# Two heads at a time, 36 chunks of layer 0 beside the choice and spread of experts, and layer 1 with 64 tokens by gathered rows

## The chip, the core and the metric

The kernel runs on one core of a Trainium2 chip. The metric is the device time of one execution in microseconds (us). The core has TensorE (PE, with its weight loads shown as PEld), VectorE (DVE), ScalarE (ACT), GpSimd (POOL) and SyncE (SP, which here only issues DMAs), and 16 DMA engines which all queues share.

## The reference

Two layers work on 256 context tokens and 256 latent tokens of 1024 values. Layer 0 mixes tokens by latent attention (8 heads) and a retention (8 heads), layer 1 by a gated delta rule. After each mixer comes a "peer" layer, a product-key mixture of 16384 experts, each one row of `u` and one row of `v`:

```python
def peer(h, w_q, k1, k2, u_tab, v_tab):          # per block of 128 tokens xb
    q = (xb @ w_q).reshape(PEER_BLOCK, PEER_HEADS, 2, half)
    s1 = jnp.einsum('phd,hnd->phn', q[:, :, 0], k1); s2 = jnp.einsum('phd,hnd->phn', q[:, :, 1], k2)
    v1, i1 = lax.top_k(s1, PEER_TOPK); v2, i2 = lax.top_k(s2, PEER_TOPK)
    ...
    sc, j = lax.top_k(cand, PEER_TOPK)            # 16 experts of each of 8 heads
    gate = jax.nn.softmax(sc.astype(F32), axis=-1)
    act = jax.nn.gelu(jnp.einsum('phkd,pd->phk', u_tab[e_idx], xb).astype(F32), approximate=False)
    return jnp.einsum('phk,phkd->pd', (gate * act).astype(xb.dtype), v_tab[e_idx])
```

So each token has 128 slots (8 heads, 16 experts). In layer 0 all 512 tokens go through `peer`, in layer 1 only the 256 latent ones.

## The kernel before

All arithmetic is float32. Where accuracy allows one pass, a factor is split into a high and a low part (`split`, L264: ScalarE rounds to the high part at L270, VectorE or GpSimd subtracts at L273), and a product is three matmuls of such parts (`mm3`, L258; each `mm` is at L256). Other products are plain f32 matmuls, which the trace shows as two instructions each.

**Layer 0's mixer** (`mixer0`). After the projections, a pipeline of eight `attend(h)` is woven with a pipeline of four `retain(hp)`. A head of attention makes queries and keys (tiles `q`, `k`), scores `s`, a softmax, transposes `pt` to `pT`, and at the end the product `oa`: 64 columns of weights (`VM`) against `pT`, so a head fills one half of the columns of the array and of the rows of the output, by h % 2. Retention takes heads in pairs, one after the other: scores `rs` with 64 rows of the array, product with a decay on VectorE to `sd`, and the product `or` with 64 columns.

**The peer layers** are done densely and by rows. Dense: the experts stand in 128 chunks of 128. For a chunk, `act` (24 matmuls, a chunk of `u` as weights, N tokens as columns) gives the activations of all tokens against all experts of the chunk, `gelu` follows, they are multiplied by the weight matrix W (zero where a token did not choose the expert), and `f` adds the product with the chunk of `v` into PSUM (per block of 128 tokens two halves of 512 columns, three matmuls each). Layer 0 does three of four token blocks so (N = 384), layer 1 both (N = 256).

W is made by `route`. *Choice*: the projections `pq`, scores `sc`, and on VectorE the top 16 of each half and of the candidates. *Spread*: `decode`, `place`, `slots`, and `spread`, which for groups of 16 tokens builds one-hot tiles `O` and `A` on VectorE and ScalarE, multiplies them (`wp`, 32 matmuls per group) and writes the result `wst` to W in DRAM. `EARLY` = 12 and 24 chunks of `act` of layers 0 and 1 are woven into the spread, and their activations stay in SBUF.

`Dense.run` then goes over pairs of chunks: `act` of both (if not early), the extra work listed in `fill` for these chunks, the loads of W (`w`, four chunks at a time) and of `vr`, `gelu` times W (L1108), splits of the activations (`gsh`, `gsl`) and of `vr` (`vsh`, `vsl`), and the products `f` of the pair before. `ur` and `vr` have two buffers each, the split `vs` three in layer 0 and four in layer 1.

*Rows* (layer 0, the last block of 128 tokens): `Rows.steps` goes over 128 slots. A step gathers one row of `u` for each of the 128 tokens by an indirect DMA of GpSimd (L1042), takes the product with the token on VectorE (L1049), and eight steps later adds the gathered row of `v` times its weight (L1059). These steps, and 56 units that compute the modulation (`ada_unit`, L343: one load of 512 KB, one or two passes of VectorE), are spread over the chunks of layer 0's loop by `fill`: steps from chunk 8 to 120, units at every second chunk from chunk 12.

The build orders the instructions of each engine; a few of a later chunk can stand ahead of their place in the code. Queues run in order: SyncE's holds the loads of `ur`, `vr`, `w` and `adat`, GpSimd's the gathers.

## Time and profile before

| what | value |
|---|---|
| time, median of 3 runs | 3143.77 us (3142.84 to 3145.04) |
| the profiled execution | 3142.63 us, of which span 3140.7 us |
| mean granted TensorE clock | 0.94 |
| busy: TensorE, VectorE, ScalarE, GpSimd | 2816.7, 2305.4, 1281.7, 708.5 us |
| DMA | 626 MB, mean 199 GB/s |

Stages in the span: layer 0's mixer to 390, choice and spread of layer 0 to 690, its dense loop to 1745, the delta rule to 2245, choice and spread of layer 1 to 2436, its dense loop to 3123, the end to 3140.7. The share of a busy engine is read per stretch: "busy" of TensorE is the time in which some matmul is open, and matmuls overlap, so the number of them in a stretch says more on the pace. The chain of work that ended last shows what each instant waited for.

### The profile page before, as it was taken

The numbers are of one execution on the slowest core, as the hardware profiler recorded it, in microseconds if no ns is written. First come the engines' busy times: TensorE is split into PE (matmuls) and PEld (weight loads), VectorE is DVE, ScalarE is ACT, GpSimd is POOL, SyncE is SP. The second block draws the span as 40 slices with busy tenths as digits, with TensorE's granted clock in tenths as the row PEclk, the third lists the DMA queues.
The fourth block names the chain that finished last, engine by engine and source line by source line (L and its number), as shares of the span: only waits on it lengthen the run. The fifth ranks groups of instructions, "written<-read, shape, count | busy, mean of one in ns | idle before, by whom it ended". The sixth has DMA issues, their size and how long they took to land.

```text
span 3140.7 us, 44585 instructions
## 1 busy us (share of the span) xinstructions
PE 2816.7 (90%) x16843; PEld 2443.3 (78%) x16843; DVE 2305.4 (73%) x4520; ACT 1281.7 (41%) x2145; POOL 708.5 (23%) x453
## 2 busy tenths in 40 slices
PE   8989895857999999999999887669887899999997
PEld 4756685746999998888999666668787689999997
DVE  2955689977999999994444587976799655555555
ACT  3234432753333333333333334322348454444443
POOL 2410130024545555540000234423310100000000
PEclk9999997978999999999999888779899899999999
DMA  6530321568999999994443122312336866667663
GB/s 229 187 108 21 114 75 61 198 245 307 378 382 380 384 397 400 400 362 156 156 156 118 57 63 78 95 48 81 115 128 237 264 216 210 213 210 213 210 213 108
DMA packets 257192, 626.02 MB, mean 199 GB/s; under 512 B 34800, under 2 KB 124016, under 8 KB 252496
## 3 DMA queue, kind: packets, MB, share of 16 engines
q1 hardware_dynamic: 217632, 478.58, 45.3%
q0 software_dynamic: 38768, 142.49, 11.7%
q8 instruction: 132, 2.16, 0.3%
q10 hardware_dynamic: 576, 2.10, 0.2%
q14 instruction: 84, 0.69, 0.1%
HBM read 574.86 MB, written 48.23 MB: 198 GB/s over the span
## 4 chain that ended last, share of the span: by engine, by line
PE 55%; DVE 27%; DMA 9%; issue 5%; ACT 3%; POOL 1%; SPq 0%; POOLq 0%; ACTq 0%; DVEq 0%
PE f L256 20%; PE act L256 20%; DMA ur<-p_u 3%; DMA vr<-p_v 3%; DVE adaj L343 2%; DVE usl L273 2%; DVE cv L1264 2%; PE dz L256 1%; DVE O L966 1%; DVE rowy L1059 1%; PE y L256 1%; DVE vsl L273 1%; DVE rowu L1049 1%; DVE gelu L1108 1%; PE s L256 1%
## 5 line engine op out<-in xcount | busy, mean ns | idle before, releaser
L256 PE MATMUL f<-vsh,gsh 128*128 128x512 f32 x1260 | 491.1, 395 | 36.0 <-ACT vsh L270 36.0
L256 PE MATMUL f<-vsl,gsh 128*128 128x512 f32 x1260 | 497.7, 395 | 12.7 <-DVE vsl L273 12.5
L256 PE MATMUL f<-vsh,gsl 128*128 128x512 f32 x1260 | 494.9, 393 | 0.0
L273 DVE TENSOR_TENSOR vsl<-vr,vsh 128x1024 fp32r<-128x1024 f32 x252 | 301.4, 1228 | 246.8 <-ACT vsh L270 246.3
L273 DVE TENSOR_TENSOR usl<-ur,ush 128x1024 fp32r<-128x1024 f32 x256 | 313.5, 1226 | 173.9 <-ACT ush L270 173.9
L270 ACT ACTIVATE vsh<-vr 128x1024 fp32r<-128x1024 f32 x252 | 256.6, 1053 | 339.1 <-PE f L256 233.9
L270 ACT ACTIVATE ush<-ur 128x1024 fp32r<-128x1024 f32 x256 | 270.4, 1056 | 280.3 <-PE act L256 210.4
L256 PE MATMUL act<-hp0h,usl 128*128 128x384 f32 x1024 | 346.0, 338 | 14.5 <-DVE usl L273 14.5
L256 PE MATMUL act<-hp0h,ush 128*128 128x384 f32 x1024 | 347.0, 339 | 0.6 <-ACT ush L270 0.6
L256 PE MATMUL act<-hp0l,ush 128*128 128x384 f32 x1024 | 345.4, 337 | 0.0
L256 PEld LDWEIGHTS f<-vsh,gsh 128*128 128x128 f32 x1260 | 239.0, 190 | 88.8 <-ACT vsh L270 42.1
L256 PE MATMUL act<-hp1h,usl 128*128 128x256 f32 x1024 | 293.6, 287 | 7.7 <-DVE usl L273 7.7
L256 PE MATMUL act<-hp1h,ush 128*128 128x256 f32 x1024 | 293.6, 287 | 5.5 <-ACT ush L270 5.5
L256 PE MATMUL act<-hp1l,ush 128*128 128x256 f32 x1024 | 292.2, 285 | 0.0
L256 PEld LDWEIGHTS f<-vsl,gsh 128*128 128x128 f32 x1260 | 239.3, 190 | 65.4 <-DVE vsl L273 19.2
L256 PEld LDWEIGHTS f<-vsh,gsl 128*128 128x128 f32 x1260 | 239.1, 190 | 49.6
L270 ACT ACTIVATE gsh<-gelu 128x384 fp32r<-128x384 f32 (+1 forms) x256 | 120.3, 471 | 376.4 <-DVE gelu L1108 342.3
L1042 POOL DMA_INDIRECT rowu<-p_ur,rowe x128 | 181.6, 1419 | 189.7 <-DVE rowa L1049 135.3
L1042 POOL DMA_INDIRECT rowv<-p_v,rowe x128 | 180.2, 1408 | 146.0 <-DVE rowy L1059 121.4
L256 PEld LDWEIGHTS act<-hp0h,usl 128*128 128x128 f32 x1024 | 193.8, 189 | 15.7 <-DVE usl L273 15.3
L256 PEld LDWEIGHTS act<-hp1h,usl 128*128 128x128 f32 x1024 | 199.1, 195 | 8.9 <-DVE usl L273 8.7
L256 PEld LDWEIGHTS act<-hp1h,ush 128*128 128x128 f32 x1024 | 198.9, 194 | 8.4 <-ACT ush L270 6.3
(770 smaller groups left out, 5970.8 us busy)
## 6 DMA issues: line engine op xcount, KB each, us to landing
ur<-p_u SPq DMA_DIRECT2D x256, 512.0 KB, 4.4
vr<-p_v SPq DMA_DIRECT2D x256, 512.0 KB, 4.4
adat<-ada_t SPq DMA_DIRECT2D x80, 512.0 KB, 7.1
W<-wst SPq DMA_DIRECT2D x20, 2048.0 KB, 7.1
w<-W SPq DMA_DIRECT2D x32, 768.0 KB, 9.5
wq<-p_wq SPq DMA_DIRECT2D x32, 512.0 KB, 3.4
dw<-dn_in SPq DMA_DIRECT2D x32, 512.0 KB, 3.4
w<-W SPq DMA_DIRECT2D x32, 512.0 KB, 5.6
```

Source lines behind the costliest of these rows:

```text
L256: self.nc.tensor.matmul(out, l, r, start=start, stop=stop)
L270: nc.scalar.activation(hi, x, AF.Copy)
L273: (eng or nc.vector).tensor_sub(lo, x, hi.bitcast(F32))
L343: nc.vector.tensor_tensor_reduce(j, w, self.crow[:, s, :], op0=ALU.mult, op1=ALU.add, scale=1.0, scalar=self.c["ada_c"][:, l, m, k:k + 1], ...
L966: nc.vector.tensor_tensor(pairs(O[:, n]), bc(n), iob.unsqueeze(1).broadcast_to([P, OH, 64, 2]), ALU.is_equal)
L1042: nc.gpsimd.indirect_dma_start(t, None, tabs[z], bass.IndirectOffsetOnAxis(ap=self.e[:, s:s + 1], axis=0))
L1049: nc.vector.tensor_tensor_reduce(u, u, self.h, op0=ALU.mult, op1=ALU.add, scale=1.0, scalar=0.0, accum_out=self.act[:, s:s + 1])
L1059: nc.vector.scalar_tensor_tensor(self.y, rows.pop((1, v)), self.g[:, v:v + 1], self.y, ALU.mult, ALU.add)
L1108: nc.vector.tensor_mul(gv, gv, w4[:, :, c % WC, :])
L1264: (nc.gpsimd if CONV[j] == "p" else nc.vector).scalar_tensor_tensor(co, xp[:, :ns, q:q + T], cw[:, j, q:q + 1], co, ALU.mult, ALU.add)
```

## The change

Three things. **Heads two by two:** `attend` of an even head stops after its transposes, and the odd head's `oa` does both heads, alternating between the halves of the array; `retain` makes `rs` and `or` of its two heads alternating. **Layer 0, 36 chunks early:** `EARLY` is 36 and 24; activations of all but the first `KEEP` = 4 early chunks are written to DRAM (`away`, ScalarE's queue) and read back in the loop (SyncE's queue). The early work now begins in the choice, once the projections are issued (`step`), where GpSimd makes the low parts; it goes on between `decode`, `place` and in `spread`; the four kept chunks come last. The next chunk's table is loaded and split while the present one is multiplied. The `fill` work of the loop is placed by shares of its cost (`paces`): the units and the affine step earlier, the row steps from about chunk 32 to the end. **Layer 1:** 192 tokens dense (`N` = P + HALF), the last 64 by rows. Both halves of the partitions hold these tokens, with slots 0 to 63 and 64 to 127, so 64 steps gather two slots at a time. Of the weighted rows every second is added on TensorE in f32 (`halves`, weights `d` made by ScalarE), the others on VectorE (`rowy`), which a last product folds. For the half block, `gs` holds high and low parts side by side, so that `f` needs two matmuls instead of three there. The tables are the same data under two names.

```diff
-EARLY = 12, 24
-LEAD = 15, 45
+EARLY = 36, 24
+KEEP = 4
-RING = 4, 3
+RING = (4, 3), (4, 3)
@@ attend(h)
-            o = ps.tile([P, T2], F32, tag="ps", name=f"oa{h}")
+            if h % 2 == 0:
+                first.append(pTs)
+                return
+            both = (first.pop(0), pTs)
...
                 for kb in range(nk):
-                    self.mm(o[rows, s * T:(s + 1) * T], VM[:, kb, h * 64:(h + 1) * 64], pTs[s][:, kb, :], kb == 0, kb == nk - 1)
-            put(h // 2, rows, o[rows])
+                    for z in range(2):
+                        self.mm(o[z * 64:z * 64 + 64, s * T:(s + 1) * T], VM[:, kb, (h - 1 + z) * 64:(h + z) * 64], both[z][s][:, kb, :], kb == 0, kb == nk - 1)
+            put(h // 2, slice(0, P), o)
@@ retain(hp)
+            for s, b0, own in ((0, 0, 0), (1, 0, 1), (1, 2, 0)):
+                os = [ps.tile([P, 2, T], F32, tag="ps", name=f"rs{hp}{z}{s}{b0}") for z in range(2)]
+                for sb in range(2):
+                    k0 = (b0 + sb) * P
+                    for z in range(2):
+                        self.mm(os[z][:, sb, :], rk[rows[z], hp, k0:k0 + P], rq[rows[z], hp, s * T:(s + 1) * T])
...
-        rest = pipe([retain(hp) for hp in range(4)], 2)
+        rest = pipe([retain(hp) for hp in range(4)], 2, 3)
@@ route
+        pd, work = dense.p, dense.early(e2, ps)
+        beside = islice(work, (EARLY[l] - KEEP) * KD // 2)
...
+        def step(n):
+            for _ in range(n):
+                next(beside, None)
...
+                if ends[0]:
+                    n += 1
+                    step(1 + n % 2)
                 yield
...
+            step(4 + 4 * l)
...
-            for gi in range(P // OH):
+            for gi in range(min(P, dense.N - tb * P) // OH):
...
-                weave(spread(tb, SHARE[l]), until=work)
+                weave(spread(tb, SHARE[l]), until=beside)
         weave(work)
@@ Rows.choose, halves, steps
+                    for r in range(0, P, self.n):
+                        for z in range(2):
+                            self.m.mm(o[r:r + self.n, i * P:(i + 1) * P], hs[z][:, 4 * h + i, ts].bitcast(F32), c["ident"], z == 0, z == 1)
...
+        def halves(self, acc, w, t, first, last):
+            for h in range(2):
+                self.m.mm(acc[h * 64:h * 64 + 64, :], w, t[:, h * 512:(h + 1) * 512], first, last)
...
+                    if acc is not None and v % 2 == 0:
+                        d = pool.tile([P, n], F32, tag="rowd", name=f"rowd{l}{v}", bufs=3)
+                        nc.scalar.activation(d, self.fold, AF.Copy, scale=self.g[:, v:v + 1])
+                        self.halves(acc, d, t, v == 0, False)
+                    else:
+                        nc.vector.scalar_tensor_tensor(self.y, t, self.g[:, v:v + 1], self.y, ALU.mult, ALU.add)
@@ Dense
+        def ahead(self, order, ps):
+            m, nc, l = self.m, self.m.nc, self.l
+            us = self.table(order[0])
+            for n, c in enumerate(order):
+                now, us = us, None
+                o = ps.tile([P, 512], F32, tag="ps", name=f"act{l}{c}")
+                for k in range(KD):
+                    self.product(o, now, k)
+                    if k == 1 and n + 1 < len(order):
+                        us = self.table(order[n + 1])
+                    if k % 2:
+                        yield
+                if c < KEEP:
+                    self.gelu(c, o)
+                else:
+                    g = self.pg.tile([P, self.N], F32, tag="gelus", name=f"gelus{l}{c}", bufs=3)
+                    nc.scalar.activation(g, o[:, :self.N], AF.Gelu)
+                    nc.scalar.dma_start(self.away[c], g)
...
+            def fetch(c):
+                late = c >= NE - 2
+                vr = (self.p if late else pool).tile([P, D], F32, tag="ur" if late else "vr", name=f"vr{l}{c}", bufs=2)
+                nc.sync.dma_start(vr, m.a[f"p_vr{l}"][c * P:(c + 1) * P])
+                if KEEP <= c < done:
+                    self.gelu(c, None)
+                return vr
...
+                        if half:
+                            for z in range(2):
+                                m.mm(acc[tb][h], gs[:, whole:whole + P], vs[z][:, hl], first and z == 0, last and z == 1)
+                        else:
+                            m.mm3(acc[tb][h], (gs[:, sl], gs[:, second(tb * P):second(tb * P) + P]), (vs[0][:, hl], vs[1][:, hl]), first, last)
@@ build
+        def paces(done, first, second):
+            cost = np.cumsum([second if c < done else first + second for c in range(NE - 6)])
+            return lambda share: int(np.searchsorted(cost, min(share, 1.0) * cost[-1]))
...
+        fill, at = {}, paces(EARLY[0], 18, 18)
+        ahead_share = EARLY[0] / (2 * (NE - 6) - EARLY[0])
         for i, u in enumerate(units):
-            fill.setdefault(12 + 2 * i, []).append(lambda u=u: m.ada_unit(pa, *u))
+            n = 3 * KD
+            share = ahead_share * (0.1 + 0.9 * i / n) if i < n else ahead_share + (0.97 - ahead_share) * (i - n) / (len(units) - n)
+            fill.setdefault(at(share), []).append(lambda u=u: m.ada_unit(pa, *u))
...
-            fill.setdefault(8 + i * 112 // (P + LAG), []).append(lambda: next(steps))
+            fill.setdefault(at(0.9 * ahead_share + (1 - 0.9 * ahead_share) * i / (P + LAG)), []).append(lambda: next(steps))
...
+            dense = m.Dense(m, 1, h, P + HALF, *pools1, EARLY[1])
...
+            fill, at = {2: [affine]}, paces(EARLY[1], 24, 20)
+            for i in range(rows.n + LAG):
+                fill.setdefault(at((i + 1) / (rows.n + LAG)), []).append(lambda: next(steps))
```

## Rows read from the trace of the kernel before

**Rows 1.** The page's part 4: shares of the chain that ended last, by engine.

```profile
PE 55%; DVE 27%; DMA 9%; issue 5%; ACT 3%; POOL 1%; SPq 0%; POOLq 0%; ACTq 0%; DVEq 0%
```

**Rows 2.** Stretches: length, busy PE, PEld, DVE, ACT, POOL (instructions), PEclk, DMA, GB/s.

```profile
196.00:331.00 135.00, 130.74 (x585) 82.60 (x585) 78.95 (x163) 60.85 (x133) 0.00 (x0) 1.00 0.14 42
495.00:690.00 195.00, 130.84 (x1145) 116.65 (x1143) 183.56 (x367) 113.52 (x252) 2.79 (x4) 0.84 0.46 175
690.00:772.00 82.00, 50.36 (x183) 38.43 (x183) 59.03 (x74) 24.57 (x33) 45.35 (x27) 0.76 0.83 291
772.00:1044.00 272.00, 271.41 (x1373) 247.20 (x1374) 271.32 (x383) 99.17 (x143) 138.12 (x98) 1.00 1.01 377
1044.00:1420.00 376.00, 365.89 (x1836) 330.01 (x1836) 356.47 (x496) 130.07 (x191) 197.89 (x139) 1.00 1.01 384
...
2304.00:2436.00 132.00, 104.20 (x981) 96.72 (x980) 127.39 (x236) 88.23 (x189) 0.58 (x1) 0.90 0.52 192
```

**Rows 3.** Groups, 196 to 331, TensorE: tile, shapes, count | busy us, mean ns.

```profile
L256 PE MATMUL rs<-rq,rk 64*128 64x256 f32 x96 | 27.6, 407 | 0.0
...
L256 PE MATMUL oa<-pT,VM 128*64 128x256 f32 x96 | 21.3, 382 | 0.0
```

**Rows 4.** Timeline of TensorE: start us, length us, instruction, count merged.

```profile
233.99 0.38 PE L256 MATMUL oa<-pT,VM 128*64 128x256 f32 x1
234.05 0.38 PE L256 MATMUL or<-sd,rv 128*64 128x256 f32 x1
234.21 0.38 PE L256 MATMUL oa<-pT,VM 128*64 128x256 f32 x1
...
237.32 2.80 PE L256 MATMUL or<-sd,rv 128*64 128x256 f32 x12
```

**Rows 5.** The chain in order of time: start us, us, matmuls packed, count.

```profile
307.66 0.86 PE gm L256 x2
403.44 0.89 PE sc L256 x8
550.57 3.41 PE wp L256 x32
846.55 8.34 PE act L256 x48
854.89 8.20 PE f L256 x36
2551.59 5.47 PE f L256 x24
2557.05 5.75 PE act L256 x48
```

**Rows 6.** The chain where layer 0's spread turns into its loop.

```profile
678.07 10.48 DMA W<-wst
...
688.62 9.00 DMA w<-W
```

**Rows 7.** Groups from 780 to 1040, the loop of layer 0, VectorE and ScalarE.

```profile
L1059 DVE SCALAR_TENSOR_TENSOR rowy<-rowv,rowg,rowy 128x1024 f32<-128x1024 f32 x48 | 61.4, 1278 | 0.0
L1049 DVE CUSTOM_DVE_ANT_0 rowu<-rowu,rowh 128x1024 f32<-128x1024 f32 x47 | 57.1, 1216 | 0.0
L343 DVE CUSTOM_DVE_ANT_0 adaj<-adat,c_row,small 128x1024 f16<-128x1024 f32 x38 | 48.5, 1277 | 0.0
...
L273 DVE TENSOR_TENSOR vsl<-vr,vsh 128x1024 fp32r<-128x1024 f32 x32 | 37.7, 1217 | 0.4 <-ACT vsh L270 0.4
...
L270 ACT ACTIVATE vsh<-vr 128x1024 fp32r<-128x1024 f32 x32 | 32.1, 1052 | 64.4 <-PE f L256 64.4
```

**Rows 8.** Groups from 395 to 490, the choice of layer 0, GpSimd.

```profile
L273 POOL TENSOR_TENSOR usl<-wq,ush 128x1024 fp32r<-128x1024 f32 x14 | 33.6, 2398 | 55.4 <-ACT ush L270 55.4
```

**Rows 9.** DMA issues, 780 to 1040, then 2550 to 3100: KB, median us to landing.

```profile
vr<-p_v SPq DMA_DIRECT2D x32, 512.0 KB, 7.4
...
vr<-p_v SPq DMA_DIRECT2D x99, 512.0 KB, 4.2
```

More of the change, by code (lines that the diff above doesn't have):

```diff
@@ L2 @@
 from contextlib import ExitStack
-from itertools import chain, count, cycle
+from itertools import chain, count, cycle, islice
 import numpy as np
@@ L638, in mixer0 @@
         p = self.pool(ea, "m0at", 3)
+        first = []
         def attend(h):
@@ L942, in slots @@
             tr = ps.tile([P, 512], F32, tag="ps", name="tr" + t)
+            ii = [place(tb, n) for n in range(2)]
             for n in range(2):
-                nc.tensor.transpose(tr[:, n * P:(n + 1) * P], place(tb, n), c["ident"])
+                nc.tensor.transpose(tr[:, n * P:(n + 1) * P], ii[n], c["ident"])
+            if rows is not None and rows.tb == tb:
+                rows.choose(g, ii, hs, ps)
             nc.tensor.transpose(tr[:, 2 * P:3 * P], g.rearrange("p h k -> p (h k)"), c["ident"])
@@ L984, in spread @@
                 yield
-        work = choose(0)
+        for part in range(len(parts)):
+            weave(choose(part))
+        eq_.close()
+        dense.by = None
         for part, tbs in enumerate(parts):
-            weave(work)
-            if part + 1 < len(parts):
-                work, lead = choose(part + 1), 2 * AHEAD
-            else:
-                eq_.close()
-                work, lead = early(), LEAD[l]
-            for _ in range(lead):
-                next(work)
             decode(part)
@@ L1058, in steps @@
                 if v >= 0:
-                    nc.vector.scalar_tensor_tensor(self.y, rows.pop((1, v)), self.g[:, v:v + 1], self.y, ALU.mult, ALU.add)
+                    t = rows.pop((1, v))
+                    if acc is not None and v % 2 == 0:
[4 more added lines that the diff above has]
+                        nc.vector.scalar_tensor_tensor(self.y, t, self.g[:, v:v + 1], self.y, ALU.mult, ALU.add)
+                    if acc is not None and v == n - 1:
+                        self.halves(acc, self.fold, self.y, False, True)
                 yield
@@ L1064, with __init__ @@
         G = 2
-        def __init__(self, m, l, hs, nb, pool, ring):
-            self.m, self.l, self.hs, self.nb, self.p, self.ring = m, l, hs, nb, pool, ring
+        def __init__(self, m, l, hs, N, pool, done):
+            self.m, self.l, self.hs, self.N, self.p, self.done = m, l, hs, N, pool, done
             self.g = {}
         def early(self, es, ps):
-            self.pg = self.m.pool(es, f"gelu{self.l}", 1)
-            return chain.from_iterable(self.act(c, ps, "ps") for c in range(self.ring))
@@ new lines, in act, with run, second @@
+        def act(self, c, ps, tag):
+            us = self.table(c)
+            o = ps.tile([P, 512], F32, tag=tag, name=f"act{self.l}{c}")
+            for k in range(KD):
+                self.product(o, us, k)
+            self.gelu(c, o)
+        def run(self, wd, pool, psa, psv, fill):
+            m, nc, l, N, G, done = self.m, self.m.nc, self.l, self.N, self.G, self.done
+            nb = -(-N // P)
+            whole = N // P * P
+            def second(t):
+                return N if t >= whole else 2 * N - whole + t
@@ L1138, in run @@
                         f()
-                for c in range(c0, c0 + G if c0 < NE - 2 * G else NE):
-                    group.append(weighted(c))
+                rows = [fetch(c) for c in cs[:G]]
+                group = [weighted(c, rows.pop(0) if rows else fetch(c)) for c in cs]
                 for tb in range(nb if todo else 0):
-                    os = products(*todo, tb)
-                    for h in range(2 if sums is not None else 0):
-                        s = sums[:, tb, h * 512:(h + 1) * 512]
-                        if todo[0] == 0:
-                            nc.vector.tensor_copy(s, os[h])
-                        else:
-                            nc.vector.tensor_add(s, s, os[h])
+                    products(*todo, tb)
```

242 lines of the change are left out of this document (132 added, 110 removed).

## The prediction, made before the result

> **What bounds the kernel now.** I read the chain that ended last first: TensorE holds 55% of it, VectorE 27%, DMA 9% [rows 1]. Then I cut the span into stretches [rows 2]: "busy" of TensorE is not its pace there, so I set against each stretch what its matmuls need when packed. Packed paces are in the chain [rows 5]: 36 `f` matmuls (512 columns) in 8.20 us, 0.228 each; 48 `act` of 384 columns in 8.34, 0.174; 48 of 256 columns in 5.75, 0.120; a plain f32 matmul runs as two instructions, 0.43 us each at 512 columns (`gm`) and 0.111 at 128 (`sc`); a half-precision `wp` of 128 columns takes 0.107.
>
> Layer 0, from the first `act` at 495 to 1745: the work is 3072 `act` x 0.174 = 534, some 2256 `f` x 0.228 = 514, 768 `wp` x 0.107 = 82, 8 of others: 1138 of 1250 us. So TensorE lacks work for 112 us only: 49 in 495 to 690 (choice and spread, where VectorE is busy 184 of 195), 40 in 690 to 772 (183 `f` = 42 of 82), 14 in 1044 to 1420, the rest small [rows 2]. From 772 to 1044 there is no gap although VectorE is busy 271 of 272 us and DMA at 377 GB/s. Layer 1, from 2304 to 3123: 3072 x 0.120 + 1536 x 0.228 + 512 x 0.107 + 3 = 776 of 819, idle 43. Attention and retention, 196 to 331: TensorE busy 131 of 135, VectorE 79, ScalarE 61 [rows 2]. Everywhere the change touches, TensorE sets the end; it counts only what shortens its work or fills its gaps.
>
> **Part 1, heads two by two.** `rs` (64 rows) and `or`, `oa` (64 columns of the array) are 96 instructions each and run alone: 0.29 us for `rs`, 0.22 to 0.23 for the others [rows 3], [rows 4]. The change lets two halves of the array alternate. The trace has an accident of that: where an `oa` of one head meets an `or`, starts follow at 233.99, 234.05, 234.21, two instructions in 0.22 us instead of one [rows 4]. `or` and `oa` then fall from 43 (96 x 0.222 and 96 x 0.23) to 22; `rs` has no such row, between 0 and half; I take half, 27.6 to 14, since its two halves read different rows and write different banks. Saved: 36 of 135; VectorE's 79 leaves room, but the chain softmax, transpose, product is as long as before, and some `oa` and `or` overlapped already, so I give back a third: **-25** (between -10 and -34). More buffers cost nothing in time.
> The Trainium skill, "TensorE: Matmul & The Clock Gate", section "The mechanism" of its Part 3, says that a weight load overlaps a running matmul only when the row groups differ, which speaks against pairs of `oa`, whose row group is the same. By it the two products would gain nothing, and this part would be some -9 (rival D holds the case). The three starts above disagree.
>
> **Part 2, 36 chunks of layer 0 early.** It moves 24 chunks of `act` (100 us of TensorE) from the loop into choice and spread. Total TensorE work stays; what can be won is its idle time of 112. What becomes of it:
> Before the spread: the code asks for 51 of the 128 quarter-chunks in the choice, 24 more up to the first `wp`, 53 in the spread; then 16 for the four kept chunks. From 495, 150 us of `act`, 82 of `wp` and 6 more need 238, so the stage ends at 733 or later, against 685 now. VectorE in the same time: the choice as now, three blocks of spread, some 22 `usl` of 1.22 instead of 12, as POOL takes those of the choice at 2.40 each [rows 8], under the 4.2 of a chunk: it is full about as long, so I leave 10 idle. The spilled activations go out on ScalarE's queue and come back on SyncE's ahead of a weight by 32 x 0.2 MB, beside some 310 GB/s (per chunk 0.52 MB of row, 0.2 of W, 0.2 of these, 0.35 of `adat`, in 4.1 us): nothing, under the 377 of [rows 2].
> Turn-over: now W is written (10.48) and read (9.00) with TensorE empty [rows 6]; the kept chunks give it 17 us of work meanwhile, I leave 15 idle.
> First 36 chunks of the loop: only `f` is left, 8.20 a pair. Here a stall is new: three buffers of split rows serve two per pair, so the fourth row is split after the pair's end: 1.05 (`vsh`, ScalarE) + 1.22 (`vsl`) [rows 7], of which 2 x 0.68 are covered by three matmuls on each side: about 1 us per pair, 17 pairs; VectorE has 4.6 of splits and weights and 2.7 passes of `adaj` of 1.28 [rows 7] in these 9.3 us, and is near full: 25 in all.
> The rest: 92 chunks, 136 row steps over some 90 of them = 1.5 per chunk. From 780 to 1040, 48 steps went over 31.4 chunks, 1.53, with 38 passes of `adaj` [rows 7] and no gap of TensorE. The new loop asks for no more, so it stays at TensorE's pace; 15 idle for its ends.
> Sum 10 + 15 + 25 + 15 = 65 against 112: **-45** (between -70 if the `f` stretch is covered, and 0 if the gaps only change place).
>
> **Part 3, layer 1.** TensorE, packed:
> `f`: 12 to 10 per chunk, 256 fewer x 0.228 = -58. `wp` of 64 tokens: 128 x 0.107 = -14. `rowt`: 64 instructions x 0.111 = +7, in the spread.
> `act` at 192 columns: no row shows this form. The line through 256, 384 and 512 columns [rows 5] gives 0.0926; no row with a weight load per matmul is under 0.107; at worst the 256 columns' 0.120 if it follows the packed rows at all. I take 0.111, the f32 row of 128 columns, nearest in what it must load: 3072 x -0.009 = -27 (-84 to 0).
> The same page, section "LDWEIGHTS (loading the stationary operand)", states columns / 1.2 ns, 107 for 128, and "Back-to-back issue gap" N / 2.4 + 2.5, 82.5 for 192. By the first the sum moves by -12, by the second by -88; `wp` at 0.107 with half the columns agrees with the first.
> Row halves: 32 weighted rows and one fold, each two f32 products of 512 columns, four instructions of 0.43 [rows 5]: 1.75 us one after another, 1.3 if the column halves overlap (the second of one beside the first of the other): +43 (to 58).
> Together -49. Idle time: 43 now. The 64 steps put two gathers of 0.52 MB each and 2.5 or 1.3 us of VectorE on every 1.5 chunks. A pair then has 5.3 + 4.6 + 0.9 = 10.8 us of TensorE; VectorE 9.2 of it; DMA 3.7 MB, 340 GB/s. A row of `vr` now lands after 4.2 us, but 7.4 at 379 GB/s [rows 9], so 6.7 here; 6.7 + 1.05 + 1.22 + one row pass of 1.28 [rows 7] is 10.3, just inside 10.8. I add 22 for pairs that miss it, and 7 at the end (copies of halves, last fold). The spread has 12 groups instead of 16 (VectorE is busy 127 of 132 us there [rows 2]); that is in the idle time, as the early chunks fill it. **-20** (between -75 and +40).
>
> **Sum.** -25 - 45 - 20 = -90. The profiled execution took 3142.6 (span 3140.7 and 1.9 around it), so 3052.6; the median of the three runs is 1.1 above it: **3054**.
>
> **Rivals.**
> A: layer 0 keeps its gaps. VectorE is busy 184 of 195 in choice and spread [rows 2]; if wp and the early `act` wait for each other, or the `f` stretch is VectorE's, the 100 us come back as wait: 3099. For it: VectorE's share; against: the two splits done by POOL. Chance 0.15.
> B: in layer 1 the round of a `vr` buffer becomes the bound. Decides above 10.8 us per pair, a landing of 7.2; at 8.4 each of 52 pairs loses 1.2: +60, 3114. For: the landing of 7.4 in layer 0; against: 340 is under 379 GB/s, and a slower loop asks for less. Chance 0.11. A and B together: 3159, slower: 0.09.
> C, slower: the 192-column `act` is not run at one column per clock but like plain f32. Its place is all 3072 of layer 1; the gain is eaten at 0.111 + 90/3072 = 0.14 us each. `oa`, f32 with 256 columns, takes 2 x 0.224, so 192 columns 0.35: +734, some 3790. For: the trace has no such matmul under 256 columns; against: 256, 384 and 512 lie on one line. Chance 0.10.
> D, the halves do not do what they should: no pair overlaps, part 1 is worth nothing, and the row halves cost 15 more: 3094. Against it is one spot of the trace only. Chance 0.05.
>
> **How the numbers follow.** The forecast has 0.50. Its own range is 3009 to 3099, from the three parts' bounds taken as independent. With A, B and D the range is 2995 to 3150; C and half of A with B stay out. A difference under 0.2% (6 us) can't be told here from none. Faster: 0.50 + 0.14 + 0.10 + 0.05 = 0.79. Within 0.2%: 0.05, from the edges of A, B, and of both. Slower: 0.10 + 0.06 = 0.16.
>
> **What would show it.** Part 1: `oa` and `or` start in pairs within 0.1 us, and the stage from 196 ends near 306. Part 2: first `f` near 745, pairs of the first 36 chunks at 9.3 us, later ones at 16.5 with no gap; a pair over 17 is A. Part 3: `act` at 0.111 (over 0.14 is C), pairs at 10.8; waits of `vsh` on DMA in every pair are B. The forecast is wrong if TensorE's matmuls are packed in a stretch and still take longer, or if its idle time from 495 on exceeds 112.

## The result: 3164.8 us, slower by 0.66%, and the profile after

The changed kernel takes 3164.8 us (median of 3162.3 to 3168.5), the kernel before 3144.4; the ratio is 1.0066, 95% interval 1.0048 to 1.0083. The forecast was 3054, range 2995 to 3150. The profiled execution has a span of 3160.6 us.

The chain that ended last, by engine (the page's part 4, shares of the span, of the kernel after):

```profile
PE 32%; DVE 15%; DMA 12%; issue 10%; POOL 7%; ACT 2%; POOLq 0%; DVEq 0%; SPq 0%; ACTq 0%
```

This row cannot be set against [rows 1] share by share: there the shares add up to 100, here to 78, as the chain is followed back only to 695 us and leaves out the mixer and layer 0's choice and spread. It says only that behind 695 the DMA (12) and GpSimd (7) hold parts of the end. Where, the stretches say (columns as in [rows 2]: length, busy PE, PEld, DVE, ACT, POOL, granted clock, DMA share, GB/s):

```profile
475.00:724.00 249.00, 217.47 (x1676) 204.55 (x1674) 217.04 (x380) 151.13 (x304) 39.63 (x22) 0.95 0.61 224
724.00:900.00 176.00, 163.95 (x684) 130.40 (x685) 156.67 (x254) 56.93 (x81) 17.43 (x12) 0.95 0.93 317
950.00:1450.00 500.00, 462.38 (x2270) 413.79 (x2269) 464.38 (x610) 160.81 (x241) 313.78 (x215) 0.97 0.99 378
1500.00:1700.00 200.00, 199.97 (x1030) 182.61 (x1029) 85.60 (x111) 72.66 (x100) 0.00 (x0) 1.00 0.45 144
2275.00:2400.00 125.00, 100.44 (x948) 96.52 (x948) 109.58 (x218) 72.28 (x157) 0.57 (x1) 0.86 0.52 189
2400.00:2500.00 100.00, 49.21 (x233) 39.97 (x231) 66.93 (x123) 25.82 (x46) 48.32 (x37) 0.73 0.92 324
2500.00:2650.00 150.00, 110.64 (x563) 91.61 (x564) 112.44 (x199) 51.18 (x89) 61.30 (x49) 0.84 0.90 313
2700.00:3100.00 400.00, 400.00 (x2648) 347.35 (x2646) 261.36 (x403) 198.05 (x324) 67.46 (x46) 1.00 0.79 278
```

Four lines stand out. The loop of layer 0 (950 to 1450), nearly packed in [rows 2], loses 38 us of 500 by TensorE's busy time, and then runs from 1500 to 1700 with no rows at all and the DMA at 144 GB/s. The first 250 us of layer 1's loop lose 51 of 100 and 39 of 150; from 2700 on nothing is lost.

By milestones: the first `pq` comes 21 us earlier than before, the first `act` of layer 0 20, the last group of layer 0's `f` 32, the first `act` of layer 1 29; from there to the last `f` it takes 865 us where it took 819.

What work the loop of layer 1 has where it is packed, in the chain of 2700 to 2760 (start us, us, matmuls, count; compare [rows 5]):

```profile
2703.47 1.01 PE yr L255 x4
2704.49 4.78 PE f L255 x20
2709.26 5.34 PE act L255 x48
2714.60 4.57 PE f L255 x20
```

`act` at 192 columns is 5.34/48 = 0.111, as taken; a row pair of halves is 1.01, under the 1.3 taken. And mixer 0, the timeline of TensorE (start us, us, tile, count merged), to be read against [rows 3, 4]:

```profile
240.86 2.81 PE L255 MATMUL oa<-pT,VM 128*64 128x256 f32 x24
...
247.62 2.81 PE L255 MATMUL or<-sd,rv 128*64 128x256 f32 x24
252.65 1.13 PE L255 MATMUL rs<-rq,rk 64*128 64x256 f32 x8
```

`oa` and `or` are 2.81/24 = 0.117 where they were 0.22, `rs` 1.13/8 = 0.141 where it was 0.29: all of them halved.

Next is VectorE by groups (busy us, mean ns | idle before it, and what ended it) in the loop of layer 0, 950 to 1450, and at the start of layer 1's, 2400 to 2650:

```profile
L1112 DVE SCALAR_TENSOR_TENSOR rowy<-rowv,rowg,rowy 128x1024 f32<-128x1024 f32 x103 | 131.8, 1280 | 24.2 <-DMA rowv<-p_vr,rowe 24.0
L1096 DVE CUSTOM_DVE_ANT_0 rowu<-rowu,rowh 128x1024 f32<-128x1024 f32 x103 | 130.2, 1264 | 0.0
L272 DVE TENSOR_TENSOR vsl<-vr,vsh 128x1024 fp32r<-128x1024 f32 x54 | 67.9, 1297 | 0.0
...
L1096 DVE CUSTOM_DVE_ANT_0 rowu<-rowu,rowh 128x1024 f32<-128x1024 f32 x64 | 79.4, 1254 | 18.2 <-DMA rowu<-p_ur,rowe 18.2
L272 DVE TENSOR_TENSOR vsl<-vr,vsh 128x1024 fp32r<-128x1024 f32 x38 | 46.9, 1244 | 33.5 <-ACT vsh L269 33.3
```

The number of `vsl` is the number of chunks. Layer 0 ran 103 row steps in 54 chunks, 1.91 a chunk, though the code asks for 1.5. Layer 1 ran all its 64 U passes in 2400 to 2650, some 36 of them in the 24 chunks of `f` alone, though the code asks for 0.3 a chunk there and 0.66 behind it. The order of an engine's queue is made when the kernel is built. No operand of a row step belongs to the chunk beside which the code puts it, so nothing holds the step there, and here the build set the steps earlier than the code asks. Neither number could be read from the code.

The last views are of the start of layer 1's loop: TensorE's longest waits from 2400 to 2650, in the form of the groups above, and a piece of the chain (start us, us, what):

```profile
L255 PE MATMUL f<-vsh,gs 128*128 128x512 f32 x204 | 76.2, 436 | 15.7 <-ACT vsh L269 15.4 <-DVE gs L1215 0.2
...
L255 PE MATMUL act<-hp1h,ush 128*128 128x192 f32 x141 | 44.4, 315 | 36.3 <-ACT gelu L1169 26.2 <-ACT ush L269 10.2
...
L255 PE MATMUL adag<-small,gcol 128*128 128x128 f32 x16 | 3.7, 374 | 28.7 <-DVE gcol L361 28.7
```

```profile
2485.97 6.27 DMA vr<-p_vr
...
2492.32 1.07 ACT vsh L269
2493.42 1.01 DVE vsl L272
```

The wait before `adag` is a single one, from 2431 to 2460, and more than half of the 51 us that 2400 to 2500 loses. `adag` makes the gate rows that layer 1 needs at its end; in TensorE's queue it stands among the first `f`, ahead of nearly all of them. Three of its small operands `gcol` stand in VectorE's queue behind eleven U passes that were drawn forward: 13.5 us of work and 8.6 of waits for their gathers. So a row pass delays TensorE here without any dense operand being late.

### The profile page after: what moved, and what is told of

Its sections match the earlier page's. It is cut to its first block, busy times and chain, and to the rows that moved or that the text cites. A ratio compares the mean times of both kernels' runs of the same rounds, so it can differ in the third digit from the quotient of the medians.

```text
span 3160.6 us, 44975 instructions
## 1 busy us (share of the span) xinstructions
PE 2772.5 (88%) x16655; PEld 2379.4 (75%) x16655; DVE 2396.8 (76%) x4797; ACT 1252.3 (40%) x2160; POOL 922.4 (29%) x598
## 4 chain that ended last, share of the span: by engine, by line
PE 32%; DVE 15%; DMA 12%; issue 10%; POOL 7%; ACT 2%; POOLq 0%; DVEq 0%; SPq 0%; ACTq 0%
PE act L255 12%; PE f L255 12%; DMA rowv<-p_vr,rowe 4%; DMA vr<-p_vr 3%; POOL rowu L1089 3%; POOL rowv L1089 3%; DVE cv L1360 2%; PE dz L255 2%; DMA ur<-p_u 1%; DMA rowu<-p_ur,rowe 1%; PE yr L255 1%; DVE usl L272 1%; DVE vsl L272 1%; DVE rowu L1096 1%; PE yo L255 1%
## 5 line engine op out<-in xcount | busy, mean ns | idle before, releaser
L255 PE MATMUL f<-vsh,gs 128*128 128x512 f32 x2268 | 754.3, 402 | 33.7 <-ACT vsh L269 23.7
L255 PEld LDWEIGHTS f<-vsh,gs 128*128 128x128 f32 x2268 | 435.3, 193 | 145.6 <-ACT vsh L269 32.5
L255 PE MATMUL f<-vsl,gs 128*128 128x512 f32 x1260 | 503.4, 402 | 37.7 <-DVE vsl L272 37.6
L1089 POOL DMA_INDIRECT rowv<-p_vr,rowe x192 | 278.7, 1452 | 489.2 <-DVE rowy L1112 296.4
L255 PE MATMUL act<-hp1h,ush 128*128 128x192 f32 x1024 | 292.6, 286 | 38.1 <-ACT gelu L1169 26.2
L255 PEld LDWEIGHTS f<-vsl,gs 128*128 128x128 f32 x1260 | 243.1, 193 | 99.2 <-DVE vsl L272 51.4
L255 PE MATMUL act<-hp1h,usl 128*128 128x192 f32 x1024 | 291.1, 284 | 22.2 <-DVE usl L272 22.2
L255 PE MATMUL act<-hp1l,ush 128*128 128x192 f32 x1024 | 290.2, 283 | 0.0
L1096 DVE CUSTOM_DVE_ANT_0 rowu<-rowu,rowh 128x1024 f32<-128x1024 f32 x192 | 240.0, 1255 | 20.0 <-DMA rowu<-p_ur,rowe 20.0
L255 PEld LDWEIGHTS act<-hp1l,ush 128*128 128x128 f32 x1024 | 206.4, 202 | 2.2
```

The lines of the kernel that those rows point to most:

```text
L255: self.nc.tensor.matmul(out, l, r, start=start, stop=stop)
L1089: nc.gpsimd.indirect_dma_start(t, None, tabs[z], bass.IndirectOffsetOnAxis(ap=self.e[:, s:s + 1], axis=0))
L1096: nc.vector.tensor_tensor_reduce(u, u, self.h, op0=ALU.mult, op1=ALU.add, scale=1.0, scalar=0.0, accum_out=self.act[:, s:s + 1])
```

## The experiments

Medians; the ratio is to the kernel before, run beside them, with its 95% interval. That kernel's own medians were 3142.1 to 3145.6 us, so differences of 3 us between two experiments say nothing.

### Which part of the change cost what

**Heads alone.** The kernel before with the new `attend` and `retain`, nothing else.

> The kernel before with the first mixer's heads two by two and nothing else of the change. The first pq of the changed kernel came 21 us earlier: 3144.4 - 21 = 3123 us (3117 to 3129). Rival: the layers behind are bound by something that does not move with the start, then 3144 us (3139 to 3149).

3122.8 us, 0.9923 (0.9906 to 0.9939): -22. In its trace the first `pq` comes 26 us earlier than before and the last `f` 19, so most of the gain lasts to the end.

**Layer 1 without its row part.**

```diff
-            dense = m.Dense(m, 1, h, P + HALF, *pools1, EARLY[1])
-            wd = m.route(1, h, ((0, 1),), ps, first, dense, e2, rows)
+            dense = m.Dense(m, 1, h, T, *pools1, EARLY[1])
+            wd = m.route(1, h, ((0, 1),), ps, first, dense, e2)
...
-            psm = m.pool(ed, "d1ps", 1, PSUM, side="right")
+            psm = m.pool(ed, "d1ps", 2, PSUM, side="right")
...
```

> The changed kernel with the row part of layer 1 undone alone: 256 tokens dense and no gathered rows there, as before; the early 24 chunks, the split by GpSimd, mixer 0 and layer 0 stay as changed. Against before, the changed kernel reaches the first act of layer 1 28.8 us earlier and then takes 45.6 us more to the last f. If the row part alone made that loss: 3144.4 - 29 = 3115 us (3108 to 3122). Rival: something else of layer 1 (the new order of the early chunks) takes a part, then 3130 or more.

3109.6 us, 0.9883 (0.9858 to 0.9908). So the row part of layer 1 (with the second PSUM buffer of the gate rows, which it had taken) costs 3164.8 - 3109.6 = 55 us net; heads and layer 0 (with what else changed in layer 1) give 35, of which the heads are 22 and the rest 13.

### Layer 1: the rows, or the round of `vr`

**No row steps in layer 1** (the calls of `next(steps)` and the use of `yr` are taken out).

> The changed kernel with 192 dense tokens in layer 1 and the row steps of layer 1 left out: no gathers, no U passes, no V products (the experts' sum of the last 64 tokens is left out). It takes away 32 of 1.01 us on TensorE in any theory. Theory 1 (the U passes and gathers, drawn into the stretch of f alone, make the idle time): idle of TensorE in the stage falls from 148 to 55, so 3164.8 - 32 - 93 = 3040 us (3025 to 3060). Theory 2 (the round of vr through its two buffers, 8.1 us a link beside 4.6 us of f, holds that stretch whatever the rows do): most idle time stays, 3164.8 - 32 - 30 = 3103 us (3085 to 3125).

3041.5 us, 0.9658 (0.9639 to 0.9678): theory 1's number. 123 us go, of which only 32 are work of TensorE. The same two stretches, without rows:

```profile
2400.00:2500.00 100.00, 73.88 (x352) 59.24 (x351) 53.99 (x108) 38.98 (x61) 12.55 (x8) 0.86 0.73 244
2500.00:3000.00 500.00, 499.12 (x3420) 458.63 (x3419) 314.92 (x505) 262.31 (x404) 0.00 (x0) 1.00 0.74 234
```

The stretch of `f` alone loses 26 of 100, not 51, and behind it nothing. Of the 25 that come back 20 are the wait before `adag`, now 8.7; 20 of the 26 that stay lie ahead of 2440. The round of `vr` alone (rival B of the prediction) is not what holds this layer: its loads land in 4.2 us here, 6.0 in 2400 to 2650 of the changed kernel.

**Row numbers released late, four slots at a time**, from chunk 24: the gather cannot start before; the pass may stand anywhere behind it.

```diff
...
+nc.vector.scalar_tensor_tensor(self.eq[i], dense.g[max(dense.g)][:, :self.q], 0.0, self.ef[:, s:s + self.q], ALU.mult, ALU.add)
...
-fill.setdefault(at((i + 1) / (rows.n + LAG)), []).append(lambda: next(steps))
+fill.setdefault(24 + i * 98 // (rows.n + LAG), []).append(lambda: next(steps))
```

> The changed kernel with the row numbers of layer 1 released four slots at a time from chunk 24 on, one group every six or so chunks (the group's numbers are written by an instruction that reads the activations of that chunk), so that no row pass can be drawn into the stretch of f alone. Nothing is left out. Theory 1 (drawn-forward passes): of the 120 us idle in 2410 to 2700 some 70 come back, 3095 us (3080 to 3115). Theory 2 (the round of vr): the stretch of f alone keeps its idle time and the later stretch gets more rows than now, 3165 us or more (3155 to 3185).

3172.0 us, 1.0074 (1.0053 to 1.0096): no gain, and theory 1 in its simple form (too early) falls. Its stretches:

```profile
2400.00:2500.00 100.00, 72.50 (x387) 60.30 (x385) 56.75 (x106) 41.36 (x66) 14.08 (x8) 0.86 0.75 250
2500.00:3000.00 500.00, 440.52 (x2695) 376.07 (x2694) 343.67 (x559) 204.65 (x350) 140.84 (x113) 0.94 0.83 296
```

VectorE's row groups and ScalarE's Gelu over row activations, 2500 to 3000 (the last figures are the idle time before the group and what ended it):

```profile
L1106 DVE CUSTOM_DVE_ANT_0 rowu<-rowu,rowh 128x1024 f32<-128x1024 f32 x60 | 72.8, 1224 | 36.1 <-DMA rowu<-p_ur,roweq 35.6
L1122 DVE SCALAR_TENSOR_TENSOR rowy<-rowv,rowg,rowy 128x1024 f32<-128x1024 f32 x26 | 33.4, 1283 | 49.1 <-DMA rowv<-p_vr,roweq 49.1
L1108 ACT ACTIVATE rowa<-rowa 128x4 f32<-128x4 f32 x15 | 3.1, 207 | 84.7 <-DVE rowa L1106 84.7
```

The `f` stretch got back 23 of its 51 (19 of them before `adag`, which waits 9.3 here), but 59 were lost from 2500 to 3000, where the changed kernel lost 39. VectorE is busy 344 of 500 us, so it is not full; but it stands 85 us at a row pass whose gather has not landed. Its queue is in order: `usl`, `vsl` and the weights behind such a pass wait too. That made theory 3.

**Passes tied to chunks, by the chunk's activation.** Now the gather may run ahead by its ring, and the pass is held back:

```diff
+z = self.z[:, 0, s:s + 1]
+nc.vector.tensor_scalar_mul(z, dense.g[max(dense.g)][:, :1], 0.0)
...
-... scale=1.0, scalar=0.0, accum_out=self.act[:, s:s + 1])
+... scale=1.0, scalar=z, accum_out=self.act[:, s:s + 1])
...
+g = self.z[:, 1, s:s + 1]
+nc.vector.tensor_add(g, self.g[:, v:v + 1], z)
```

> The changed kernel with every row pass of layer 1 (not its gather) tied to the chunk at which the code asks for it, 0.73 a chunk from chunk 24 on: a column that is nought times an activation of that chunk goes into the U pass as its scalar and is added to the weight of the V product. The gathers stay four and three slots ahead, so each has some 30 us or more before its pass. Nothing is left out. Theory 3 (in VectorE's queue the passes stand ahead of the landing of their gathers; it waits at the queue's head, 85 us for rowu and rowv in 500 us of the run with paced numbers, and the splits behind it are late): the idle time falls to about that of the run without rows, so its 3041.5 + 32 of yr = 3074 us (3062 to 3095). Theory 4 (the load of the row part itself, VectorE 0.7 busy and the DMA at 0.8, wherever it is put): 3165 us (3150 to 3180).

3202.0 us, 1.0173 (1.0153 to 1.0193): slower. By itself it would speak for theory 4, but its trace (2500 to 3000) has another wait:

```profile
L1101 DVE CUSTOM_DVE_ANT_0 rowu<-rowu,rowh,rowz 128x1024 f32<-128x1024 f32 x56 | 72.0, 1285 | 2.0
L1121 DVE SCALAR_TENSOR_TENSOR rowy<-rowv,rowz,rowy 128x1024 f32<-128x1024 f32 x24 | 30.7, 1279 | 0.0
L255 PE MATMUL yr<-rowv,rowd 128*64 128x512 f32 x96 | 31.5, 740 | 54.2 <-ACT rowd L1118 54.2
```

The waits for gathers are gone, and TensorE now stands 54 us ahead of `yr`, for `rowd`, which waits for a column made from TensorE's own newest `act`. The experiment had put in a wait of its own and told nothing of the two theories.

**The same tie, by the chunk's `usl`**, which VectorE itself wrote:

```diff
-nc.vector.tensor_scalar_mul(z, dense.g[max(dense.g)][:, :1], 0.0)
+nc.vector.tensor_scalar_mul(z, dense.low[:, 0, :1].bitcast(F32), 0.0)
```

> As l1_gate, but the column that ties a pass to its chunk is nought times an entry of that chunk's usl, which VectorE wrote itself a little earlier, and not of its activation: in l1_gate the tie was a wait of its own (TensorE stood 54 us in 500 ahead of yr, for rowd, which waited for a column made from TensorE's own newest act). Passes at 0.73 a chunk from chunk 24 on, gathers ahead by the ring. Nothing is left out. Theory 3 (passes ahead of the landing of their gathers in VectorE's queue): 3041.5 + 32 = 3074 us, with a little for the ties 3085 (3065 to 3105). Theory 4 (the load of the row part): 3165 us or more (3150 to 3200).

3088.6 us, 0.9823 (0.9791 to 0.9854): -76 against the changed kernel, theory 3's number. Its stretches:

```profile
2400.00:2500.00 100.00, 68.57 (x318) 55.61 (x317) 60.85 (x112) 35.71 (x56) 23.24 (x15) 0.83 0.83 285
2500.00:3000.00 500.00, 495.28 (x3245) 428.19 (x3244) 409.90 (x761) 251.44 (x419) 141.32 (x118) 1.00 0.94 337
```

VectorE's row groups from 2500 to 3000:

```profile
L1101 DVE CUSTOM_DVE_ANT_0 rowu<-rowu,rowh,rowz 128x1024 f32<-128x1024 f32 x61 | 78.4, 1285 | 2.2
L1121 DVE SCALAR_TENSOR_TENSOR rowy<-rowv,rowz,rowy 128x1024 f32<-128x1024 f32 x31 | 39.8, 1285 | 0.6
```

The gathers in the same time (tile, queue, operation, count, median us from issue to landing):

```profile
rowv<-p_vr,rowe POOLq DMA_INDIRECT x61, 8.1
rowu<-p_ur,rowe POOLq DMA_INDIRECT x57, 6.3
```

VectorE is busier (410 against 344), the DMA faster (337 against 296 GB/s), and TensorE idle for 5 us instead of 59; VectorE's waits for gathers fell from 85 to 3. Both runs start at chunk 24 with nearly the same number of steps; what differs is that here the gather may start earlier and its pass is held back. The load of the row part (theory 4) is not the cause.

**The tie without the late start**: the chunks that the changed code asks for.

> As l1_low (passes of layer 1 tied by usl), but at the chunks at which the changed kernel's code asks for them, spread over the whole loop by work, 0.3 a chunk in the stretch of f alone, in place of a start at chunk 24. Nothing is left out. If the ties alone are the remedy: 3088 us (3078 to 3098). If rows in the stretch of f alone cost by themselves, whatever their pace: 3105 us or more.

3103.3 us, 0.9867 (0.9844 to 0.9891). The ties give 61 of the 76 us, the late start 15. PE busy in 2400 to 2500 is 60.2 here and 68.6 in the run before; 7 of these 8 us are the wait before `adag`, 17.7 here and 10.7 there. A count says that the stretch has no room for rows besides: a chunk with `f` alone needs 4.57/2 = 2.29 us of TensorE, and VectorE's own part is 1.22 (`vsl`) + 0.35 (weights) + 2 x 0.25 (`gs`) = 2.1; a single pass of 1.25 would make VectorE the bound. No run tests this count apart from `adag`.

**By which way the wait reaches TensorE.** In 2650 to 3100 of the changed kernel VectorE stands 79 us for `rowv` and TensorE is packed, so a wait at the queue's head is not always paid. One candidate was ScalarE, where the Gelu over four row activations stands ahead of the dense one. It was left out in layer 1, in the paced kernel and in the changed one.

```diff
-                    if s % 4 == 3:
+                    if s % 4 == 3 and l == 0:
```

> l1_paced with the Gelu over each four row activations left out in layer 1 (so the gathered tokens' weights lack their activation function); VectorE's order is the same as in l1_paced. Theory 5 (the passes' wait reaches TensorE over ScalarE: in l1_paced the Gelu of the rows stands 84.7 us in 500 at the head of ScalarE's queue for its U passes, the Gelu of the dense chunk behind it is late, and act waits 51.6 us for its PSUM buffer): 3172 - 50 = 3122 us (3105 to 3138). Rival (VectorE's own queue: passes ahead of the landing hold usl and vsl): 3170 us (3160 to 3180).

> The changed kernel with the same Gelu left out in layer 1 and nothing else; VectorE's order is the same. In 2400 to 2650 act waits 26 us for the dense Gelu and 10 for ush, f 15 for vsh, all on ScalarE, where the rows' Gelu stands 43.5 us for the U passes. Theory 5: 3164.8 - 35 = 3130 us (3118 to 3142). Rival (VectorE's own queue, or vr landing late): 3165 us (3157 to 3172).

3154.3 us, 1.0041 (1.0021 to 1.0061), and 3162.7, 1.0061 (1.0043 to 1.0079): -18 and -2 us, or -10 and -2 by the ratios, and the two ratios of the paced kernel overlap at their edges. So ScalarE is a small part of it at most in the paced kernel, and none in the changed one. The wait changed its name (paced without that Gelu, ScalarE, 2500 to 3000; with it this row had 183.6):

```profile
L1222 ACT ACTIVATE gs<-gelu 128x192 fp32r<-128x192 f32 x80 | 29.1, 363 | 253.4 <-DVE gelu L1219 253.4
```

ScalarE waits for VectorE's weights instead, which points back at VectorE's queue. Why the 79 us behind 2650 are free is not settled. What the rows show there: no U pass is left, and VectorE is busy 261 of 400 from 2700 on.

### Layer 0: the affine, the place, the density

**The affine on GpSimd put back to chunk 2.**

```diff
-        fill.setdefault(at(0.4), []).append(affine)
+        fill.setdefault(2, []).append(affine)
```

> The changed kernel with the affine of layer 0 (two loads and eight passes on GpSimd) put back from 0.4 of the loop to chunk 2, ahead of the gathers, as before. Theory A (in GpSimd's queue it holds up the gathers behind it, which cost about 32 us in 940 to 1140): 3164.8 - 27 = 3138 us (3130 to 3147). Theory B (the loss there is the density of the row steps, 1.88 a chunk, and the DMA at 395 GB/s): 3165 us (3158 to 3172).

3153.4 us, 1.0026 (1.0011 to 1.0042): -11, between the two. The stretch from 1000 to 1100 of the changed kernel:

```profile
1000.00:1100.00 100.00, 78.13 (x355) 68.52 (x354) 87.44 (x97) 26.16 (x40) 67.92 (x43) 0.88 0.83 309
```

The affine among GpSimd's groups there:

```profile
L422 POOL TENSOR_TENSOR x<-x,lb 128x1024 f32<-128x1024 f32 x4 | 12.7, 3194 | 5.5 <-DMA lb<-ln_b 5.5
L421 POOL TENSOR_TENSOR x<-x,lg 128x1024 f32<-128x1024 f32 x4 | 10.1, 2529 | 6.7 <-DMA lg<-ln_g 6.7
```

The same stretch with the affine early:

```profile
1000.00:1100.00 100.00, 97.20 (x484) 87.71 (x483) 94.09 (x127) 33.35 (x50) 59.99 (x44) 0.98 1.03 396
```

The hole of 22 us at the affine is gone. Two things made it, and this run moves both. 35 us of GpSimd's queue, its two loads included, stood between the gathers, and VectorE stood 11 us for `rowv`. And VectorE's passes were longer beside those of the affine (the changed kernel, GpSimd and VectorE, start us, us):

```profile
1021.52 2.64 POOL L421 TENSOR_TENSOR x<-x,lg 128x1024 f32<-128x1024 f32 x1 [6.66 <-DMA lg<-ln_g]
1021.83 3.41 DVE L272 TENSOR_TENSOR usl<-ur,ush 128x1024 fp32r<-128x1024 f32 x1
...
1054.54 12.67 POOL L422 TENSOR_TENSOR x<-x,lb 128x1024 f32<-128x1024 f32 x4 [5.48 <-DMA lb<-ln_b]
...
1058.30 6.65 DVE L272 TENSOR_TENSOR vsl<-vr,vsh 128x1024 fp32r<-128x1024 f32 x2
```

An `usl` or `vsl` takes 1.22 us elsewhere. In these 100 us VectorE's passes took some 15 us more than their usual times add up to, and TensorE's waits there, 14 for `vsl` and 8 for `usl`, are all for VectorE. At chunk 2 the affine is not free either: from 724 to 900 TensorE is busy 153.2 us, 164.0 in the changed kernel, which is why only 11 of the 22 arrive. From 950 to 1450 TensorE is busy 481.6 of 500, still 18 short.

**Passes of layer 0 tied by the activation**, and **both layers so** (with the affine at chunk 2). Asked: 1.58 a chunk.

> The changed kernel with the row passes of layer 0 tied in the same way to the chunks, 1.58 a chunk over chunks 36 to 121 in place of the 1.88 measured; the affine on GpSimd stays at 0.4 of the loop. Nothing is left out. Theory B (the density: the DMA stands at 395 GB/s from 900 to 1450 and the vr tiles are late by it): the DMA falls to about 330 GB/s and of the 57 us idle in 940 to 1540 some 30 come back, 3135 us (3125 to 3145). Theory A (the affine in GpSimd's queue): the hole at the affine stays, 3155 us or more (3150 to 3165).

> Both row parts tied to their chunks, and the affine of layer 0 at chunk 2. Nothing is left out. If the three act apart (layer 1 -90 by theory 3, layer 0's density -30, its affine -11 as measured, of which the two in layer 0 may share some): 3164.8 - 120 = 3045 us (3028 to 3065), below both kernels. If theory 4 holds for layer 1: 3125 us (3110 to 3140).

3162.3 us, 1.0049 (1.0033 to 1.0066), and 3191.1, 1.0131 (1.0109 to 1.0154). The flaw is that of the first tie: VectorE stands 28 us in 500 for the activation that it ties to. They tell nothing of the theories.

**Passes of layer 0 tied by `usl`**, 1.58 a chunk, affine at chunk 2.

> The changed kernel with the row passes of layer 0 tied by usl to their chunks, 1.58 a chunk, and the affine on GpSimd at chunk 2. Nothing is left out. Theory B (density: DMA at 395 to 400 GB/s over 900 to 1450): from the 3153.4 us of the early affine some 25 come back, 3128 us (3118 to 3140). Rival (in this layer VectorE at 0.87 busy makes usl and vsl late wherever the passes stand): 3153 us (3145 to 3165).

3119.7 us, 0.9916 (0.9897 to 0.9935): -45 against the changed kernel, -34 against the affine alone.

**The same at 1.97 a chunk.**

```diff
-fill.setdefault(36 + i * 86 // (P + LAG), []).append(lambda: next(steps))
+fill.setdefault(36 + i * 69 // (P + LAG), []).append(lambda: next(steps))
```

> As l0_low (passes of layer 0 tied by usl, affine at chunk 2), but the code asks for them at 1.97 a chunk, denser than the 1.88 that the changed kernel reached. Nothing is left out. Theory B (the density: VectorE near 0.95 and the DMA near 400 GB/s): the gain of the ties goes, 3150 us (3140 to 3160). Theory 3 (the place: what hurt in this layer too was passes queued ahead of their landing, 24 us of VectorE at the queue's head for rowv in 500): the gain stays, 3122 us (3115 to 3132).

3192.1 us, 1.0143 (1.0124 to 1.0162): worse than the changed kernel. The stretch from 950 to 1450 at 1.58:

```profile
950.00:1450.00 500.00, 495.29 (x2499) 450.35 (x2499) 469.94 (x800) 177.77 (x262) 262.95 (x192) 1.00 0.99 371
```

Two of VectorE's groups in it:

```profile
L1121 DVE SCALAR_TENSOR_TENSOR rowy<-rowv,rowz,rowy 128x1024 f32<-128x1024 f32 x96 | 122.9, 1280 | 4.1 <-DMA rowv<-p_vr,rowe 3.5
...
L272 DVE TENSOR_TENSOR usl<-ur,ush 128x1024 fp32r<-128x1024 f32 x60 | 73.0, 1217 | 17.3 <-ACT ush L269 17.3
```

The same stretch at 1.97:

```profile
950.00:1450.00 500.00, 456.31 (x2179) 404.44 (x2178) 446.74 (x774) 155.46 (x232) 262.85 (x203) 0.96 0.98 358
```

And the same two groups:

```profile
L1121 DVE SCALAR_TENSOR_TENSOR rowy<-rowv,rowz,rowy 128x1024 f32<-128x1024 f32 x102 | 130.4, 1279 | 37.9 <-DMA rowv<-p_vr,rowe 37.8
...
L272 DVE TENSOR_TENSOR usl<-ur,ush 128x1024 fp32r<-128x1024 f32 x52 | 62.9, 1217 | 0.0
```

Only the density differs between the two, and it can be counted per chunk (one `usl` each). TensorE needs 18 x 0.228 + 24 x 0.174 = 8.28 us. VectorE is busy 469.9/60 = 7.83 at 1.6 steps: TensorE is the bound. It is busy 446.7/52 = 8.59 at 1.97 tied, and 464.4/54 = 8.60 at the 1.91 of the changed kernel, and waits 0.73 and 0.45 more for `rowv`: VectorE is the bound. Some 0.3 of the 8.60 are the passes made longer by the affine: with the affine early and no tie it is 468.6/56 = 8.37 at 1.93 steps. The amount of DMA is not the bound: at 371 GB/s TensorE is packed, at 358 it is not. The count gives the direction and not the whole size: that untied run at 1.93 took 3153.4 us, 39 less than the tied one at 1.97, and VectorE stood 12 us for `rowv` in it, not 38. Why the tie costs at this density is not settled.

**No row steps in layer 0.**

> The changed kernel with the row steps of layer 0 left out: no gathers, no U and V passes there (the experts' sum of its last 128 tokens is left out). It prices what they cost TensorE in this layer. If all idle time behind the stretch of f alone (57 us in 940 to 1540) is theirs: 3164.8 - 57 = 3108 us (3098 to 3116). If the affine and the modulation rows cost by themselves: 3125 us or more. If the stretch of f alone gains too (22 us): 3086 us.

3098.0 us, 0.9852 (0.9831 to 0.9873): -67, between the first and the last number. Taking the rows out altogether gives 22 us more than placing them well, but 15 of these lie in 724 to 900 (TensorE busy 172.1 against 157.0), where the affine runs in the other kernel and not in this one.

### Both remedies: a version below both kernels

Both row parts tied by `usl`, layer 1 from chunk 24, layer 0 at 1.58 a chunk, the affine at chunk 2; nothing else of the changed kernel is touched.

> Both row parts tied to their chunks by usl, and the affine of layer 0 at chunk 2. Nothing is left out. Theories 3 and B together: 3164.8 - 80 - 37 = 3048 us (3030 to 3070). Theory 4 for layer 1 with B for layer 0: 3130 us (3115 to 3165). Neither: 3153 us or more.

3040.1 us, 0.9677 (0.9638 to 0.9716): 3.2% under the kernel before.

## Why the prediction was wrong, point by point

Two of its steps failed, both idle time beside row steps: 15 us for "the rest" of layer 0 (some 58 measured) and 72 for layer 1 (some 148).

- **What bounds the kernel.** Right for the kernel before, and wherever TensorE is packed in the changed kernel the packed paces of [rows 5] hold to the second digit. "Everywhere the change touches, TensorE sets the end" no longer held once the steps stood closer: at 1.9 a chunk VectorE has more work per chunk than TensorE (8.4 to 8.6 us against 8.28).
- **Part 1, -25.** Right, and for its reason: -22 alone. `rs` at half was the choice made without a row; it measured 0.141 against 0.29. The trace's accident in [rows 4] was the better guide than the rule of the Trainium skill, "TensorE: Matmul & The Clock Gate", Part 3, section "The mechanism", that a load overlaps only when row groups differ: `oa` pairs share their row group and run at 0.117. The measurement decides. Rival D is out.
- **Part 2, -45.** The change gave about -13. Choice and spread with the early chunks were better than forecast: from 475 to 724 the work of 238 us leaves 11 idle, where 10 before the spread and 15 at the turn-over were taken. The stretch of `f` alone (724 to 900) lost 22 for 25 taken, its matmuls counted at their packed paces. The step that failed is "the rest": 136 steps over 90 chunks, 1.5 a chunk, no more than the 1.53 of [rows 7], 15 idle. By the same count (1186 `f` x 0.228 + 1558 `act` x 0.174 = 541 us of 600) it lost some 58 from 940 to 1540. The 1.53 was a pace reached, where that code asked for 1.21; the 1.5 was a pace asked, and 1.91 was reached. VectorE was 271 of 272 busy in [rows 2] at 1.53, with 38 passes of `adaj` beside; the prediction had that row in hand and gave the new density no price. The affine was not costed at all: 11 us net. The change moved it later, from chunk 2 to about chunk 59 (0.4 of the loop's cost), and not earlier, as the section on the change has it. Rival A named the right engine for the wrong place.
- **Part 3, -20.** The change gave +55. Work was right, and rather better: `act` at 0.111 as taken (rival C out), row halves 1.01 for 1.3. In this the trace, 0.111, agrees with the Trainium skill, "TensorE: Matmul & The Clock Gate", section "LDWEIGHTS (loading the stationary operand)", 107 ns for 128 columns, and not with the estimate of 82.5 worked out from its section "Back-to-back issue gap", whose formula is for a matmul by itself. The step that failed is the idle time: 72 taken, some 148 measured. It spread 64 steps evenly, one "on every 1.5 chunks", and counted a pair of 10.8 us with `act` and `f`. In fact all U passes ran in the first 250 us, over half of them in chunks of `f` alone, where VectorE has 0.2 us free by count and where 28.7 us went in one wait for `gcol` behind them. Rival B had the place: from 2486 to 2520 the chain does go round `vr`, with landings of 5.3 to 6.4, `vsh` 1.07 and `vsl` 1.2, where a pair of `f` alone needs 4.57. But its condition, a landing above 7.2 us, was not met, and without the rows the same two buffers lose nothing from 2500 on.
- **The sum.** -22 - 13 + 55 = +20, as measured, by construction: the 13 is what the other two leave. With the passes placed and the affine early: -22 for the heads, -13 - 45 = -58 for layer 0, +55 - 76 = -21 for layer 1, against the -25, -45 and -20 forecast; together 3043, measured 3040. This sum was tested, as the two remedies were run together. The terms of work were sound; the assumption under two terms of idle time, that the build would put the row steps where the code asks, was not, and no rival stood for it. "A and B together", 3159, comes near the measured 3165 by luck: choice, spread and the stretch of `f` alone in layer 0 lost less than forecast, and B's condition was not met. The range had an error of its own: the three parts' bounds, taken as independent, give about 2993 to 3130 and not 3009 to 3099; 3165 lies outside both.

## What to carry to other kernels

A side job that shares VectorE with the main loop has to be counted per chunk against TensorE's time in every stage of the loop, the thinnest first, and by the pace that the built order reaches, not by the one that the code asks for. An instruction on in-order queues needs two things: work issued early enough (the gather), and its own place held back behind the landing; a data tie from something that the same engine wrote does the second for two small instructions of VectorE a step, 0.14 and 0.15 to 0.19 us, while a tie to another engine's newest result is a new wait. At too high a density the tie did not help either (3192.1 us at 1.97 a chunk). And small work that the main loop waits for, like `gcol`, must not stand behind the side job in the same queue.

## What the runs showed of the hardware

- Two products in the two column halves of the array, with the same rows, overlap nearly fully: `oa` and `or` 0.117 us each for 0.22, `yr` 1.01 for four f32 instructions of 0.43.
- VectorE's passes that ran beside a pass of the affine on GpSimd took 2.75 to 3.93 us (`usl` 3.41, `rowu` 3.41 and 3.93, `adaj` 3.41, `gs` 2.75). In the run with the affine elsewhere the same forms take 1.22, 1.22, 1.29 and 0.55 on the mean in the same stretch. So each lost 2.1 to 2.7 us, about the length of one pass of the affine (2.4 to 3.2); what the two contend for no run shows.
- The DMA carried 371 GB/s in layer 0 and 337 in layer 1 beside a packed TensorE (495 us of 500 in both), with gathers landing in 6 to 9 us: a high DMA share was no sign of a bound here.
